# Moving the 28 KB tile of a streamed channel shuffle from the end to fourth place

## The chip, the cores and the metric

One core of one Trainium2 chip. The metric is the device time of one execution in microseconds (us), median over repeated runs. Tile sizes in KB are per partition: "a 38 KB tile" is 128 partitions of 38 KB, 4.98 MB.

## The reference

Within each pixel's 256 channels, 8 groups of 32 are interleaved. The values do not change, only their places.

```python
x = x.reshape(16, 64, 64, 8, 32)      # groups, channels per group
x = x.transpose(0, 1, 2, 4, 3)
return x.reshape(16, 64, 64, 256)     # float32: 67.11 MB in, 67.11 MB out
```

## The kernel before

The tensor is cut into slots; a slot is one tile. SyncE issues the loads, VectorE copies from a load buffer to a store buffer in shuffled order, ScalarE issues the stores. There are two load buffers and three store buffers. The first tile is loaded, copied and stored in three parts (4, 8 and 16 KB).

```python
_SLOTS = [[4, 8, 16]] + [[38]] * 12 + [[28]]
_IN_BUFS = 2
_OUT_BUFS = 3
# ... (pools, shapes)
for parts in _SLOTS:
    in_tile = in_pool.tile([P, biggest * c], F32, name="in_tile")
    out_tile = out_pool.tile([P, biggest * c], F32, name="out_tile")
    # ... (pieces: size, first row, columns)
    for q, start, cols in pieces:
        nc.sync.dma_start(out=in_tile[:, cols], in_=rows(x_flat, start, q))
    for q, start, cols in pieces:
        nc.vector.tensor_copy(
            out=out_tile[:, cols].rearrange("p (i j g) -> p i j g", j=CPG, g=G),
            in_=in_tile[:, cols].rearrange("p (i g j) -> p i j g", g=G, j=CPG),
        )
        nc.scalar.dma_start(out=rows(out_flat, start, q), in_=out_tile[:, cols])
```

Of the kernel before, what the change touches and what calls it, by code (L numbers as in the profile page):

```python
# [1 line left out]

# [4 lines left out]


F32 = mybir.dt.float32
P = 128  # L10

_SLOTS = [[4, 8, 16]] + [[38]] * 12 + [[28]]
_IN_BUFS = 2
_OUT_BUFS = 3


@with_exitstack
def kernel(
    ctx: ExitStack,
    tc: tile.TileContext,  # L20
    x: bass.AP,
    groups: bass.AP,
    out: bass.AP,
):
    nc = tc.nc
    b, h, w, c = x.shape
    G = int(groups)
    CPG = c // G
    assert G * CPG == c
    assert sum(map(sum, _SLOTS)) * P == b * h * w  # L30
    biggest = max(map(sum, _SLOTS))

    x_flat = x.rearrange("b h w c -> (b h w c)")
    out_flat = out.rearrange("b h w c -> (b h w c)")

    in_pool = ctx.enter_context(tc.tile_pool(name="in_pool", bufs=_IN_BUFS))
    out_pool = ctx.enter_context(tc.tile_pool(name="out_pool", bufs=_OUT_BUFS))

    def rows(flat, first, q):

        return flat[first * c : (first + P * q) * c].rearrange("(p f) -> p f", p=P)

    ctx.enter_context(tc.manual_schedule(engines=None))
    first = 0
# [3 lines that stand above are left out]
        at = 0  # L48
        pieces = []
        for q in parts:  # L50
            pieces.append((q, first, slice(at * c, (at + q) * c)))
            first += P * q
            at += q
# [7 lines that stand above are left out]
            nc.scalar.dma_start(  # L61
                out=rows(out_flat, start, q), in_=out_tile[:, cols]
            )


# [1 line left out]
_INS = ['x', 'groups']  # L67
_OUTS = [((16, 64, 64, 256), 'float32')]

_NUMBERS = {'groups': 8}  # L70


# [26 lines left out]
```

## Time and profile before

| | before |
|---|---|
| median of 3 runs | 316.44 us (316.36 to 316.44) |
| profiled span | 314.5 us |
| VectorE busy | 120.0 us, 38% |
| bytes moved | 134.22 MB, mean 427 GB/s |

The profile shows the span in slices with the busy tenths of the DMA engines, the packets of each DMA queue, and the groups of instructions. In the lines of a DMA queue, q1 is the loads and q10 the stores; the columns are packets, MB, and the time that the packets took as a share of 16 engines. Packets are counted where they begin, so a short stretch can show a little over 100%. The lines themselves stand in the prediction.

### The profile page before, as it was taken

The page shows a single profiled execution, that of the slowest core. Times are in us where ns is not written, and L with a number is a line of the kernel's source. Part 1 is how long each engine was busy: PE and PEld are TensorE (multiplying, and loading weights), DVE is VectorE, ACT ScalarE, POOL GpSimd, SP SyncE. Part 2 cuts the span into 40 slices and gives each one's busy share as a digit, 9 for nine tenths or more (in the row PEclk, how much of TensorE's full clock was granted, in tenths as well). Part 3 has the DMA queues.
Part 4 walks back from the last instruction along what each step waited for, and adds up shares of the span by engine and source line. Part 5 has one row for each costly group of instructions (what it writes and reads, how often), then busy time and mean ns, then how long its engine had stood idle before and what let it go on. Part 6 is the DMA issues. An engine that isn't in the chain of part 4 may idle for free.

```text
span 314.5 us, 131 instructions
## 1 busy us (share of the span) xinstructions
DVE 120.0 (38%) x16; POOL 0.2 (0%) x4
## 2 busy tenths in 40 slices
DVE  3407474290280380470560550640730830823400
POOL 0000000000000000000000000000000000000000
DMA  8999999999999999999999999999999999999997
GB/s 315 448 410 445 417 396 479 401 455 416 445 426 436 436 401 470 396 475 396 475 396 475 396 475 396 470 401 455 416 450 421 436 436 411 477 392 454 406 431 343
DMA packets 4609, 134.22 MB, mean 427 GB/s; under 512 B 513, under 2 KB 513, under 8 KB 769
## 3 DMA queue, kind: packets, MB, share of 16 engines
q1 hardware_dynamic: 2304, 67.11, 49.9%
q10 hardware_dynamic: 2304, 67.11, 49.4%
q14 instruction: 1, 0.00, 0.0%
HBM read 67.11 MB, written 67.11 MB: 427 GB/s over the span
## 4 chain that ended last, share of the span: by engine, by line
DMA 74%; DVE 19%; SPq 0%; issue 0%; DVEq 0%
DMA in_tile<-in_x_dram 74%; DVE out_tile L57 19%; SPq L55 0%; DVEq L57 0%
## 5 line engine op out<-in xcount | busy, mean ns | idle before, releaser
L57 DVE COPY out_tile<-in_tile 128x9728 f32<-128x9728 f32 (+4 forms) x16 | 120.0, 7501 | 174.7 <-DMA in_tile<-in_x_dram 174.7
L80 POOL MEMSET const-bfloat16-1.0<- 128x1 bf16 x1 | 0.1, 102 | 0.0
L80 POOL MEMSET const-uint8-127<- 128x1 uint8 x1 | 0.1, 102 | 0.0
L80 POOL MEMSET const-float32-0.0<- 128x1 f32 x1 | 0.1, 99 | 0.2 <-issue 0.2
L80 POOL MEMSET const-float32-1.0<- 128x1 f32 x1 | 0.1, 99 | 0.0
## 6 DMA issues: line engine op xcount, KB each, us to landing
in_tile<-in_x_dram SPq DMA_DIRECT2D x12, 4864.0 KB, 36.9
out_dram<-out_tile ACTq DMA_DIRECT2D x12, 4864.0 KB, 48.2
in_tile<-in_x_dram SPq DMA_DIRECT2D x1, 3584.0 KB, 33.9
out_dram<-out_tile ACTq DMA_DIRECT2D x1, 3584.0 KB, 19.0
in_tile<-in_x_dram SPq DMA_DIRECT2D x1, 2048.0 KB, 10.9
out_dram<-out_tile ACTq DMA_DIRECT2D x1, 2048.0 KB, 33.2
in_tile<-in_x_dram SPq DMA_DIRECT2D x1, 1024.0 KB, 5.4
out_dram<-out_tile ACTq DMA_DIRECT2D x1, 1024.0 KB, 24.2
```

The lines of the kernel that those rows point to most:

```text
L57: nc.vector.tensor_copy(out=out_tile[:, cols].rearrange("p (i j g) -> p i j g", j=CPG, g=G), in_=in_tile[:, cols].rearrange("p (i g j) -> ...
L80: nc = _bacc.Bacc("TRN2", target_bir_lowering=False, num_devices=1)
```

## The change

The intent: with a smaller tile in the second load buffer, that buffer is copied out sooner and its next load is issued sooner. The sizes, and so the bytes, stay the same; one load, one copy and one store move from last to fourth.

```diff
-_SLOTS = [[4, 8, 16]] + [[38]] * 12 + [[28]]
+_SLOTS = [[4, 8, 16], [28]] + [[38]] * 12
```

## The prediction

> **What bounds the kernel now.** I read the page first: the busy shares, the DMA queues and the issues.
>
> ```profile
> span 314.5 us, 131 instructions
> DVE 120.0 (38%) x16; POOL 0.2 (0%) x4
> DMA  8999999999999999999999999999999999999997
> ...
> q1 hardware_dynamic: 2304, 67.11, 49.9%
> q10 hardware_dynamic: 2304, 67.11, 49.4%
> ```
>
> The reader is to see that VectorE, the only compute engine at work, is idle for 62% of the span, while the DMA row is full from the first slice to the last. Loads (q1, issued by SyncE) and stores (q10, issued by ScalarE) each take half of the 16 DMA engines: 49.9 + 49.4 = 99.3% of the span. Each queue has 2304 packets for 16 transfers, 144 a transfer: 128 rows (one per partition) and 16 tiny ones. So a row of a tile is one packet whatever its size, and each DMA engine gets 8 rows of each transfer.
>
> Then the table of stretches, to see where the missing 0.7% lies (columns: stretch, its length, VectorE busy, GpSimd busy, clock, DMA share, GB/s).
>
> ```profile
> 0.00:1.72 1.72, 0.00 (x0) 0.20 (x4) 1.00 0.00 0
> 1.72:313.40 311.68, 120.01 (x16) 0.00 (x0) 1.00 1.00 431
> 313.40:314.50 1.10, 0.00 (x0) 0.00 (x0) 1.00 0.00 0
> 61.20:268.00 206.80, 79.85 (x9) 0.00 (x0) 1.00 1.00 434
> ```
>
> It lies at the two ends: 1.72 us before the first packet and 1.10 us after the last. Between them the share is 1.00. The DMA engines are the bound, and there is no hole in the middle to be closed.
>
> The page's chain says "DMA in_tile" 74% and the copies 19%. It follows the last copy backwards through the two load buffers and does not show that those loads stood in a full queue, so I do not read the copies as a cost. The timeline of the copies, start and last, with what they waited for:
>
> ```profile
> 12.60 3.87 DVE L57 COPY out_tile<-in_tile 128x4096 f32<-128x4096 f32 x1 [4.04 <-DMA in_tile<-in_x_dram]
> 25.93 8.95 DVE L57 COPY out_tile<-in_tile 128x9728 f32<-128x9728 f32 x1 [9.47 <-DMA in_tile<-in_x_dram]
> 41.57 8.87 DVE L57 COPY out_tile<-in_tile 128x9728 f32<-128x9728 f32 x1 [6.68 <-DMA in_tile<-in_x_dram]
> 61.31 8.87 DVE L57 COPY out_tile<-in_tile 128x9728 f32<-128x9728 f32 x1 [10.87 <-DMA in_tile<-in_x_dram]
> ...
> 288.10 6.58 DVE L57 COPY out_tile<-in_tile 128x7168 f32<-128x7168 f32 x1 [11.17 <-DMA in_tile<-in_x_dram]
> ```
>
> Every copy begins when its load lands and none waits for a store (the view of waits has no such entry). At the end, the view of DMA issues for the last 60 us gives 28.2 us to landing for the last 38 KB store and 19.0 us for the 28 KB one. They were issued at 276.96 and 294.70 (the end of their copies), so they landed at 305.2 and 313.7: the last store stood behind the one before it for 10.5 us.
>
> **What the Trainium skill says.** (1) "DMA: Bandwidth & Descriptors", section "Queues, rings and completion order": each DMA engine goes round the queues that have work, one whole packet from each. This trace agrees. In a steady stretch of one period (93.1 to 116.1 us) the DMA view counts the same packets for both queues:
>
> ```profile
> q1 hardware_dynamic: 144, 4.98, 50.1%
> q10 hardware_dynamic: 144, 4.98, 50.1%
> ```
>
> and from 12.6 to 25.9 us, where loads have 38 KB rows and stores 4 and 8 KB rows, again 144 each, though bytes differ:
>
> ```profile
> q1 hardware_dynamic: 144, 4.98, 86.9%
> q10 hardware_dynamic: 144, 0.85, 15.3%
> ```
>
> So loads and stores advance row against row, not byte against byte. (2) The same page, "Where 436 GB/s comes from": a ceiling of 435.2 GB/s for these 16 engines. The trace's steady 434 is at it, so no rate is left to win. (3) "SBUF — State Buffer", section "SBUF: two separate sides": a DMA is not slowed by a compute operation. The trace agrees as far as it goes: DMA share 1.00 with VectorE busy 39% of that stretch.
>
> **The change part by part.** Nothing is removed or added: the same 16 loads, copies and stores of the same sizes, the same two load and three store buffers; the instruction order moves one copy, one load and one store from last to fourth.
>
> *Cost of a row.* 50.1% of 16 x 23.0 us over 128 rows is 1.44 us for a 38 KB row. In the stretch 276 to 277 us, 16 rows of 28 KB took 106.2% of 16 us, 1.06 us each. The moved tile is 8 + 8 rows on each DMA engine, 17.0 us, before and after. Sum: 0.
>
> *The start.* Landing times here and below are the issue times of the timeline plus the time to landing of the DMA view over short windows. The 16 KB load lands at 12.6. Before, the next load (38 KB) landed at 25.9. After, it has 28 KB rows: 8 x (1.44 - 1.06) = 3.0 us less, with the same 8 small store rows between, so about 22.9. Its copy takes 6.6 us in place of 8.95: done near 29.6, not 34.9. So the second buffer is free, and its next load issued, 5.3 us sooner. That is the intent, and it comes true. But the load for the first buffer was issued at 16.5, when the 16 KB copy ended, and it occupies the queue: from 25.9 to 41.55 before (15.6 us), from 22.9 to 38.5 after. The sooner load waits in the queue 8.9 us (38.5 - 29.6) where it waited 6.6 (41.55 - 34.9). Nothing was starving; the head start is spent standing in line. Gain: 0.
>
> *The middle.* Period 23.0 us, as before; loads all land some 3 us earlier, because 3 us of load work has not left the queue's total but stores now do it later. How far stores lie behind loads is kept in rows. The seventh load landed at 84.2, and the fourth and fifth stores at 72.65 and 95.67, so 4.5 stores were through: a lag of 2.5 transfers, 20 rows per engine. The first three transfers each way (4, 8 and 16 KB) set this lag, and they do not change. A store buffer is reused after three tiles: before, the store issued at 93.1 landed 48.5 us later, at 141.6, and the copy that needs its buffer began at 153.3, a margin of 11.7 us. The tightest new place, the fourth copied tile, needs the 16 KB store landed. That comes near 38.5 + 4 x (1.44 + 0.61) = 46.7, against a load landing near 56.7 (19.7 us after the last before, now less 4 x 0.38 for four 28 KB store rows). No wait appears. Cost: 0.
>
> *The end.* With the last load landed, 20 store rows remain per engine. Before: 12 x 1.44 + 8 x 1.06 = 25.8 us, measured 288.0 to 313.7. After: 20 x 1.44 = 28.8 us, so the last load must land near 313.7 - 28.8 = 284.9. Its copy takes 8.9 and ends near 293.8. The 12 rows ahead of its store last until 284.9 + 17.3 = 302.2. The longer last copy therefore still has 8.4 us to spare (10.5 before). Cost: 0.
>
> Sum: 0, so 316.4 us, the median of before.
>
> **The rivals.** *A serial end.* If the last load, copy and store were a bare chain, the larger last tile would cost 8.9 - 6.6 = 2.3 us of copy and 8 x 0.38 = 3.0 us of store: 321.7. Against it: the stores waiting in front of the last one; the DMA share while the last copy ran (288.0 to 294.7) is 1.06, so full. *A starved load queue at the start.* If the engines sat idle until the second buffer came free, up to 5.3 us would be won: 311.1. Against it: from 12.6 to 25.9 the two queues' shares sum to 102%, and from 25.9 to 41.5 to 97.5%, so at most 0.4 us is there. *A store-buffer wait takes over.* If the lag grew by more than 4 rows, copies would wait for stores; the load queue would drain, yet the stores would run in its place, so it costs little unless both queues are empty. Nothing lengthens the lag: 316 to 318. *The edges of the transfers.* Larger rows at the very end can leave the 16 engines finishing less evenly, by up to one row's difference, 0.4 us; small rows pair otherwise at the start: 316.8.
>
> **Range and chances.** Three runs of before span 0.08 us. The edges are worth about 0.4 us either way, and another sitting may differ by as much, so 316.4 with 315.6 to 317.2. Two per cent is 6.3 us: more than the idle of both ends together, and to lose as much the last copy would have to lie bare. Faster 0.01, same 0.98, slower 0.01.
>
> **What would show it right or wrong.** Right: DMA share 1.00 from about 1.7 us to about 1 us before the end, 2304 packets a queue; the fourth copy starts near 22.9 and takes 6.6; its buffer's next load is issued near 29.6 and lands near 56.7; the last copy starts near 285 and ends near 294; still no copy waits for a store. Wrong: a DMA slice below 9 in the middle or during the last copy, a copy waiting for out_dram, or a row of 38 KB that takes another time than 1.44 us.

## The result, and the profile after

After: median 316.4 us (316.21 to 316.45, 6 runs); before in the same rounds 316.4 us (316.26 to 316.72, 6 runs). The ratio is 0.9998, 95% interval 0.9985 to 1.0011: the same.

The page of after, first its busy shares, DMA row and queues:

```profile
span 314.7 us, 131 instructions
DVE 119.4 (38%) x16; POOL 0.2 (0%) x4
DMA  8999999999999999999999999999999999999997
...
q1 hardware_dynamic: 2304, 67.11, 49.8%
q10 hardware_dynamic: 2304, 67.11, 49.4%
```

Nothing that bounds the kernel has moved: the DMA row is the same digit for digit, and the two queues still fill the span. The timeline of the copies of after (start, length, what ended the idle time before) shows what did move:

```profile
12.76 3.88 DVE L57 COPY out_tile<-in_tile 128x4096 f32<-128x4096 f32 x1 [4.31 <-DMA in_tile<-in_x_dram]
23.09 6.59 DVE L57 COPY out_tile<-in_tile 128x7168 f32<-128x7168 f32 x1 [6.45 <-DMA in_tile<-in_x_dram]
38.75 8.78 DVE L57 COPY out_tile<-in_tile 128x9728 f32<-128x9728 f32 x1 [9.07 <-DMA in_tile<-in_x_dram]
56.97 8.94 DVE L57 COPY out_tile<-in_tile 128x9728 f32<-128x9728 f32 x1 [9.44 <-DMA in_tile<-in_x_dram]
...
285.28 8.83 DVE L57 COPY out_tile<-in_tile 128x9728 f32<-128x9728 f32 x1 [14.19 <-DMA in_tile<-in_x_dram]
```

The second buffer was free at 29.7 us instead of 34.9. Its next load was issued there and landed at 56.9; before, issued 5.2 us later, it landed at 61.2. From the seventh load to the fifteenth, each lands 5.8 us sooner than the same load in order of before: some 3 us because the fourth load has 28 KB rows, and some 3 us because the eight rows of the 28 KB store now stand between them. The last load has 38 KB rows again and gives 3 us back (its copy starts at 285.3, before at 288.1). And the last store lands at 313.9 us, before at 313.7: the rest is paid back in the stretch of stores alone at the end, which has one 38 KB store where a 28 KB one stood.

The table of stretches of after (stretch, length, VectorE busy, GpSimd busy, clock, DMA share, GB/s) shows that no hole opened, not during the last copy either (packets that began just before a stretch are not counted in it, so 0.98 is still full):

```profile
1.72:313.50 311.78, 119.41 (x16) 0.00 (x0) 1.00 1.00 430
285.30:294.10 8.80, 8.80 (x1) 0.00 (x0) 1.00 0.98 425
```

And the DMA view of one steady period of after (110.2 to 133.2 us), with the time from issue to landing of the one load and the one store issued in it:

```profile
q1 hardware_dynamic: 144, 4.98, 50.1%
q10 hardware_dynamic: 144, 4.98, 50.1%
...
in_tile<-in_x_dram SPq DMA_DIRECT2D x1, 4864.0 KB, 37.1
out_dram<-out_tile ACTq DMA_DIRECT2D x1, 4864.0 KB, 48.5
```

These are the figures of before (37.0 and 48.5): both are issued when a copy ends, and a store lands 11.4 us, half a transfer, after a load. That half transfer turned out to matter, as the experiments show.

### The profile page after: what moved, and what is told of

It is laid out like the page before. It is cut to its first block, busy times and chain, and to the rows that moved or that the text cites. A ratio compares the mean times of both kernels' runs of the same rounds, so it can differ in the third digit from the quotient of the medians.

```text
span 314.7 us, 131 instructions
## 1 busy us (share of the span) xinstructions
DVE 119.4 (38%) x16; POOL 0.2 (0%) x4
## 4 chain that ended last, share of the span: by engine, by line
DMA 74%; DVE 19%; SPq 0%; issue 0%; DVEq 0%
DMA in_tile<-in_x_dram 74%; DVE out_tile L57 19%; SPq L55 0%; DVEq L57 0%
## 5 line engine op out<-in xcount | busy, mean ns | idle before, releaser
L57 DVE COPY out_tile<-in_tile 128x9728 f32<-128x9728 f32 (+4 forms) x16 | 119.4, 7463 | 174.7 <-DMA in_tile<-in_x_dram 174.7
```

The source lines that it names most:

```text
L57: nc.vector.tensor_copy(out=out_tile[:, cols].rearrange("p (i j g) -> p i j g", j=CPG, g=G), in_=in_tile[:, cols].rearrange("p (i g j) -> ...
```

## The experiments

The theory: the DMA engines are full from 1.7 us to the end, so the order of tiles is free as long as neither end lies bare. Rival A: the zero is a gain at the start and an equal loss at the end. Rival B: the last load, copy and store are a bare chain. Rival D: the start is on the path, as the intent of the change has it. All medians below stand against 316.3 us of before on the same chip, taken in the same rounds.

### The two halves of the change apart

`e1_end_only` has the start of before and the end of after; `e2_start_only` has the start of after and the end of before.

```diff
 # e1_end_only
-_SLOTS = [[4, 8, 16]] + [[38]] * 12 + [[28]]
+_SLOTS = [[4, 8, 16]] + [[38]] * 6 + [[28]] + [[38]] * 6
 # e2_start_only
+_SLOTS = [[4, 8, 16], [28]] + [[38]] * 5 + [[10]] + [[38]] * 6 + [[28]]
```

> The start of before with the end of after: the 28 KB tile stands in the middle (eighth), the 38 KB ones last. Theory (the DMA engines are full, order is free): 316.4 us, within 0.5 of before; the last copy 8.8 us, starting near 285. Rival A (the sooner second buffer won some us and the larger last tile lost as many, so the change's zero is a sum of two): slower than before by what the start was worth, 3 to 5 us. Rival B (bare serial end): 321.7.

> The start of after with the end of before: 4, 8, 16, then 28 KB in the second buffer, one 38 KB tile cut into a 10 KB tile in the middle and a 28 KB tile at the end. Theory: 316.4 us, at most 0.5 more for the extra 10 KB rows. Rival A (gain at the start, loss at the end): faster than before by 3 to 5 us, since only the gain is left.

Measured: 316.30 us (ratio 1.0006, interval 0.9992 to 1.0020) and 316.46 us (1.0012, 1.0000 to 1.0025). Neither half is worth anything by itself; rival A, which needs 3 to 5 us on each side, falls. In `e1_end_only` the last copy started at 285.1 us and took 8.8, as said.

### How much the end can bear

The last copy is done twice. The result stays right; only the last store is issued later.

```diff
+            for _ in range(2 if t == len(_SLOTS) - 1 else 1):
                 nc.vector.tensor_copy(...)
```

> Before with its last copy (28 KB, 6.6 us) done twice, result unchanged. Theory (reserve at the end): the copy then ends at 294.7 + 6.6 = 301.3, while store rows in front of it last until about 304.5, so nothing is lost: 316.4 to 316.9. Rival B (the last copy is bare): plus 6.6, 323.

> After with its last copy (38 KB, 8.8 us) done twice, result unchanged. Theory: the copy ends at 294.1 + 8.8 = 302.9, the rows in front of its store ran out near 301.7; with about 1 us from issue to first row the engines idle some 2 us: plus 1.5 to 3.5, so 318 to 320. Rival B (bare): plus 8.8, 325. Rival C (the end is covered whatever is done): plus 0.

Measured: on before 316.38 us (ratio 1.0005, 0.9990 to 1.0020), on after 318.34 us (1.0066, 1.0051 to 1.0081). The timeline and two stretches of the second:

```profile
285.19 17.80 DVE L58 COPY out_tile<-in_tile 128x9728 f32<-128x9728 f32 x2 [14.23 <-DMA in_tile<-in_x_dram]
...
1.72:302.00 300.28, 127.31 (x17) 0.00 (x0) 1.00 1.00 430
301.70:303.90 2.20, 1.28 (x1) 0.00 (x0) 1.00 0.29 124
```

The rows in front of the last store run out at 301.7 us, while the copy ends at 303.0 and the first row of its store begins at 303.9 (counted from the packets): some 2.2 us without work, and only there does the DMA share fall. Of 8.8 us more copy, 2.1 us show, so the reserve at the end of after is 6.7 us; of 6.6 us more on before, none. Rival B asked for all of it, rival C for none. So the end has a reserve in both kernels, and the change makes it smaller: it uses up some of what was free.

### How much the copies weigh

The shuffle is left out (wrong result), which makes every copy of after faster.

```diff
-                out=out_tile[:, cols].rearrange("p (i j g) -> p i j g", j=CPG, g=G),
-                in_=in_tile[:, cols].rearrange("p (i g j) -> p i j g", g=G, j=CPG),
+                out=out_tile[:, cols], in_=in_tile[:, cols]
```

> Wrong result on purpose: after with the copies in plain order, no shuffle, so VectorE writes with unit steps. Theory: whatever the copies then take (perhaps half of 8.8 us, perhaps the same), the time stays 316.4 within 0.4, because copies lie beside full DMA queues. Rival (the chain's 19% of copies is on the path): faster by the copies saved, up to 6 us if the first and last count, up to 50 us if the whole 19% does.

```profile
L57 DVE COPY out_tile<-in_tile 128x9728 f32<-128x9728 f32 x12 | 62.7, 5227 | 201.8 <-DMA in_tile<-in_x_dram 201.8
```

That line is the group of the twelve large copies in this run: 62.7 us in all, 5227 ns of one, where after has 8.7 to 9.0 us. The time was 316.66 us (ratio 1.0011, 0.9998 to 1.0025). Some 50 us of VectorE work taken away are worth nothing. The 19% that the page's chain gives to the copies are no cost.

### How much the start can bear

The copy out of the second load buffer is made longer: by 2.9 us on after (12 of its 28 KB copied again), by its full length on before and on after.

```diff
 # e12_after_second_late
+            for part in [cols, slice(0, 12 * c)] if t == 1 else [cols]:
 # e5_before_second_x2, e6_after_second_x2
+            for _ in range(2 if t == 1 else 1):
                 nc.vector.tensor_copy(...)
```

> After with 12 of the 28 KB copied twice in the second buffer's tile: 2.9 us of delay, its buffer free at 32.6 in place of 29.7, with a measured 2.3 us from issue to the first row 34.9, before the load queue runs out (36.5 to 37.8). Theory (slack at the start): no row is delayed, the lag stays 20 rows, 316.4 within 0.5. Rival D (the start is on the path): plus 2.9. Rival F (any disturbance of the start upsets the phase): plus 10 or more.

> Before with the copy out of the second buffer (38 KB, 8.9 us) done twice. Theory: the buffer is free at 34.9 + 8.9 = 43.8; the load queue runs out at 40.6 and the 16 KB store rows left, at full rate, at about 43.0; some 2 us idle: plus 1 to 3.5. Rival D (the start is on the path, as the change intends): plus 8.9. Rival E (start of no account at all): plus 0.

> After with the copy out of the second buffer (28 KB, 6.6 us) done twice. Theory: free at 29.7 + 6.6 = 36.3, before the load queue runs out at 37.8: plus 0 to 0.4. Together with the run on before: the change buys slack at the start and no time. Rival D (on the path): plus 6.6.

`e12_after_second_late` took 316.32 us (1.0004, 0.9991 to 1.0016). Its buffer's next load was issued at 32.66 us, so more than half of the 5.2 us won by the change was given away at no price. That is direct evidence against rival D.

The two full doublings went wrong for the theory and for every rival: 330.17 us on before (1.0436), 338.66 us on after (1.0731), more than the added copy itself (8.9 and 6.6 us). The table of stretches of `e5_before_second_x2` tells where:

```profile
42.00:47.00 5.00, 5.00 (x2) 0.00 (x0) 1.00 0.73 197
60.00:268.00 208.00, 74.82 (x9) 0.00 (x0) 1.00 1.00 413
```

The hole that I had expected is there, from 42 to 47 us: by this view 1.4 us of idle engines (27% of 5), and 1.8 us if each packet is counted for as long as it lasts. But the loss goes on for the rest of the run: DMA share 1.00 and yet 413 GB/s, where before has 434. Over 208 us that is 208 x (1 - 413/434) = 10 us. The DMA view of one period (119.1 to 143.1 us) shows in what:

```profile
q10 hardware_dynamic: 144, 4.98, 52.6%
q1 hardware_dynamic: 144, 4.98, 48.0%
...
in_tile<-in_x_dram SPq DMA_DIRECT2D x1, 4864.0 KB, 39.2
out_dram<-out_tile ACTq DMA_DIRECT2D x1, 4864.0 KB, 39.4
```

A store row takes 52.6% of 16 x 24.0 us over 128 rows, 1.58 us, in place of 1.44; a load row still 1.44. And load and store now land together (39.2 and 39.4 us after a common issue), where before they land 11.4 us apart. While the load queue was empty, the stores caught up from 20 rows behind the loads to 16, exactly two transfers.

In `e6_after_second_x2` I had the reserve too large. The copy ended at 37.7 us (the load before it had landed at 24.5, in after at 23.1), the next load was issued at once, and yet the DMA view from 39 to 40 us has not one load packet:

```profile
DMA packets 23, 0.38 MB, mean 377 GB/s; under 512 B 0, under 2 KB 0, under 8 KB 0
...
q10 hardware_dynamic: 23, 0.38, 87.8%
```

The first row of that load came at 40.0 us, 2.3 us after its issue; I had allowed about 1. Meanwhile the stores, at 0.61 us for a 16 KB row, ran the same four rows ahead. From there on the loads and stores of this run land together as well. It loses more than `e5_before_second_x2` partly at its end: while its last copy ran (311.2 to 320.0 us) the DMA share was 0.50, some 4 us of idle engines. With the stores four rows nearer and the engines no longer level, the reserve at the end is used up too; how much each of the two adds is not shown.

### A coarser start

> The 4, 8 and 16 KB first tile is replaced by one of 28 KB; 28, twelve of 38, 28. Theory in numbers: each DMA engine has 2 x (96 rows of 1.439 + 16 rows of 1.062 us) = 310.3 us of rows against 312.2 us measured for before (99.3% of 314.5), so about 1.9 us less: 314.5, range 314.2 to 315.4, although the first store can only begin near 18 us and not at 9. Rival (small first tiles are needed so that stores begin early): slower by up to 9 us.

```diff
-_SLOTS = [[4, 8, 16]] + [[38]] * 12 + [[28]]
+_SLOTS = [[28]] + [[38]] * 12 + [[28]]
```

I hoped for a version that beats both kernels, since every small row carries some extra. Measured: 328.43 us (ratio 1.0393, 1.0372 to 1.0415). The rival, that late first stores leave the engines idle, is not what the profile shows: the start is full. Its stretches, and its DMA view of one period (92.3 to 116.44 us):

```profile
1.72:36.00 34.28, 15.44 (x2) 0.00 (x0) 1.00 1.02 422
60.00:268.00 208.00, 77.25 (x9) 0.00 (x0) 1.00 1.00 414
```

```profile
q10 hardware_dynamic: 144, 4.98, 52.3%
...
in_tile<-in_x_dram SPq DMA_DIRECT2D x1, 4864.0 KB, 39.3
out_dram<-out_tile ACTq DMA_DIRECT2D x1, 4864.0 KB, 39.5
```

It is the same picture as above with no copy delayed and no queue dry: stores 16 rows behind, both landing together, store rows of 1.58 us.

### Three attempts to set the phase on purpose

The new theory: what counts, beside full engines, is the phase between the two queues. When the rows of a load and of a store run in step, store rows are slower. To move the phase alone, I cut one transfer into pieces over fewer partitions, so that each DMA engine gets a few rows more for the same bytes.

```diff
 # e9_coarse_shifted: the first load of the coarse start; e10_before_shifted: the store of tile 3
+cuts = [(0, 64, 0, half), (0, 64, half, n), (64, P, 0, n)]   # partitions, columns
 # e11_ladder: the stores of tiles 3, 5, 7 and 9
+cuts = [(0, 16, 0, half), (0, 16, half, n), (16, P, 0, n)]
```

> The coarse start (28, twelve of 38, 28) again, but its first load is cut into three pieces that give each DMA engine 12 rows in place of 8, the same bytes. New theory (phase): in the slow runs so far loads and stores cross a transfer's border together, 16 rows apart, and store rows take 1.58 us in place of 1.44; four more load rows put the stores 20 rows behind, as before and after have it, so store rows go back to 1.44, the period from 24.1 to 23.0 and the time to 314.2 to 315.6. Rival (the late first stores, or the missing small tiles, cost the time): stays near 328.

> Before with the store of its fourth tile cut into three pieces (12 rows per engine in place of 8, same bytes). No copy is delayed and no queue runs dry. Phase theory: from there on stores are 16 rows behind, store rows take 1.58 us, nine periods of 24.1 in place of 23.0: plus 9 to 12, so 325 to 329. Rival (the doubled copies lost their time by idle engines alone): 316.4 to 317.

> Before with one more store row per engine at each of the tiles 3, 5, 7 and 9 (a store cut so that an engine has 9 rows), so stores are 20, 19, 18, 17 and 16 rows behind in turn. Phase theory: store rows take 1.44 us in the first stage and 1.58 in the last; what they take at 19, 18 and 17 is not known: if only the exact meeting of rows counts they stay at 1.44 until the last stage, so plus 2 to 4; if nearness counts they rise step by step, plus 5 to 8. Rival (no phase effect): 1.44 throughout, 316.4 to 317.

None of the three gave the clean test. `e9_coarse_shifted` ran from 324.79 to 343.24 us (its profile is of a slow run). Its first load crawled. The DMA view of its first 12 us, then that of `e8_coarse_start` in the same 12 us:

```profile
DMA packets 177, 2.32 MB, mean 194 GB/s; under 512 B 32, under 2 KB 32, under 8 KB 32
```

```profile
DMA packets 160, 4.29 MB, mean 358 GB/s; under 512 B 16, under 2 KB 16, under 8 KB 16
```

Half the rate with half the partitions: the Trainium skill states it ("SBUF — State Buffer", section "Door 1: The DMA port swizzle": partitions 0 to 63 reach only half of the DMA ports), and this run agrees, 194 against 358 GB/s. With that slow start the phase that I wanted did not come about; the landings, which wait for the slowest of the 16 engines, came together here too.

`e10_before_shifted` took 321.54 us (1.0165, 1.0152 to 1.0178), between the two expectations, and so confirms neither. Its stores ended 2.7 to 2.9 us, one pair of rows, behind a load's landing, not in step, and its store rows stayed at 1.44. My expectation had the direction wrong: more store rows put the stores further behind, toward 24 rows and not 16. A load and a store issued together (at 160.5 us) land 35.0 and 60.8 us later, 25.8 us or 9 pairs of rows apart: 25 rows, one past three whole transfers. About 2 of the 5.2 us lost went while the cut pieces ran (418 GB/s from 85 to 140 us, in before 435); the rest is not placed. `e11_ladder`, one run at 331.07 us, mixes several phases with slow 16-partition pieces; nothing follows from it.

What the runs show together, counted from the packets of each trace (38 KB rows begun between 130 and 250 us; the gap is from the landing of a load, that is of its slowest engine, to the next landing of a store):

| run | gap, us | store rows over 1.5 us | median, us |
|---|---|---|---|
| before, after | 11.3 to 11.5 | 0% | 316.4 |
| `e4_after_last_x2` | 13.1 to 13.2 | 0% | 318.3 |
| `e12_after_second_late` | 11.3 to 11.5 | 0% | 316.3 |
| `e7_plain_copy` | 10.3 to 10.5 | 0% | 316.7 |
| `e10_before_shifted` | 2.7 to 2.9, once 5.2 | 0% (5.5% of load rows) | 321.5 |
| `e8_coarse_start` | 0.2 | 93% | 328.4 |
| `e5_before_second_x2` | 0.2 | 99.5% | 330.2 |
| `e6_after_second_x2` | 0.2 | 65% | 338.7 |
| `e9_coarse_shifted` | 0.2 | 5.5% | 324.8 to 343.2 |

In every run of the table whose transfers land together, some or nearly all store rows are slow; with a gap over 10 us none is. The pages of these runs say where the time went (a queue's share times the span): against before, the stores take 10.4 us more of each engine's time in `e5_before_second_x2`, 10.6 in `e8_coarse_start` and 11.0 in `e6_after_second_x2`, of 13.8, 11.6 and 20.4 us more span. In the last, loads take 3.2 us more as well, and 6.2 us more are idle.

Two runs hold a control within them. The packets do not name their engine, but each begins within 5 ns of the end of another, so they can be strung into 16 chains, one for each engine (where two packets end together the chains can be swapped, so a few rows are put to the wrong one). In `e8_coarse_start`, 15 engines have a load and a store cross the border of a transfer together, and 573 of their 576 store rows between 130 and 250 us are slow. The 16th crosses them a row or two apart; of the 59 rows outside the step 39 are not slow, nearly all of them one engine's. In `e9_coarse_shifted` it is the other way round: one engine is in step, with 35 of 44 store rows slow; the other 15 cross a row or two apart, with 2 slow rows of 625. That one engine's transfers take 24.1 us where the first to finish need 23.0, and at the end the rest wait for it. So in the same run, at the same time and with the same tiles, the engines that are in step have the slow store rows; a row or two out of step is enough to be free of them (in `e10_before_shifted`, one row out, 5.5% of the load rows are slow instead).

**What stays open.** The link between phase and slow store rows rests on these comparisons, between runs of different make and between the engines of two runs (the profile of `e9_coarse_shifted` is of a run classed slow); no run set the phase and nothing else. Nor do the runs tell whether the two rows meet in the same SBUF partitions or in HBM. A later test should shift the phase with full 128-partition transfers, by the sizes of the first tiles.

## Why the prediction was right, point by point

*The bound.* It held: DMA share 1.00, steady 433 GB/s in after. `e7_plain_copy` shows it from the other side, with VectorE's work cut from 119.4 to 70.8 us and the time unchanged.

*The start.* Predicted for the fourth copy 22.9 us and 6.6 long, for the next load 29.6, for its landing 56.7. Measured 23.1, 6.59, 29.7 and 56.9. `e2_start_only` and `e12_after_second_late` confirm that the head start has no price. The slack, however, is bounded, and below it lies a cliff that the prediction did not see.

*The middle.* The period is 23.0 us and no copy waits for a store. One statement was off: the loads land 5.8 us earlier from the seventh on, not "some 3 us"; the eight 28 KB store rows, which the estimate of 56.7 counts in part, were left out of it. Nothing rested on it, since the last load again has 38 KB rows. The prediction said that the lag of 20 rows is set by the first three transfers and does not change. That was right, and it was the step that bore the most weight: with a gap of 11.4 us in both kernels, store rows stay at 1.44 us. I had thought of the lag only as room in the store buffers. Its rival "a store-buffer wait takes over" spoke of a longer lag and found it cheap unless both queues are empty; a shorter one, 16 rows, cost over 10 us with full queues in `e5_before_second_x2` and `e8_coarse_start`. Had the change moved the lag to 16 rows, the time would have been some 4% longer, as in these two, and by the prediction's own working nobody would have seen why. That the lag is kept was reasoned; that 20 rows is a good one was luck.

*The end.* Predicted: last copy near 285 to 294, 8.4 us to spare until the store rows in front of it end at 302.2. Measured: 285.3 to 294.1, the store before the last landed at 302.4. `e4_after_last_x2` uses the reserve up and then pays 2.1 us, in the range of 1.5 to 3.5 expected from it. So the mechanism held and the reserve was a little too large: 6.7 us in place of 8.4, since the rows ran out at 301.7 and a store's first row begins 0.9 us after its copy ends.

*The chances.* Both medians lie at 316.4 us, and the ratio's interval is within 0.2% of one. The reason given for "slower 0.01", that for a loss of 2% the last copy would have to lie bare, does not hold: `e5_before_second_x2` lost 13.9 us with a DMA share of 1.08 during its last copy (307.7 to 314.3 us).

## What to carry to other kernels

Where the DMA share is 1.00 from end to end, a load issued sooner only waits longer in its queue: look for idle DMA time before you reorder, and test both ends apart, for two nothings are a stronger finding than one zero. Before you call a start or an end free, measure its reserve by lengthening one copy until it shows. And compare not only the DMA share but the time per row: engines at 1.00 moved 434 GB/s in one kernel and 413 in another, and the sign to look for was loads and stores landing together.

## What the Trainium skill lacked or had wrong

- "DMA: Bandwidth & Descriptors", section "Queues, rings and completion order", has the round-robin between queues right (144 packets each in a period) but nothing on rows in step: in four runs whose loads and stores land within 0.2 us of each other, up to 99.5% of the 38 KB store rows take about 1.58 us in place of 1.44, and in `e5_before_second_x2` and `e8_coarse_start` the period is near 24.1 us in place of 23.0. Engines of the same run that are not in step keep 1.44. Where the two rows meet is not known.
- The same page, section "Latency and other measured facts", gives some 600 ns from a sync or scalar queue's issue to the first byte. With the other queue busy, the load issued at 37.7 us in `e6_after_second_x2` had its first row at 40.0, 2.3 us later. With both queues empty, the first load of before had its first row 1.0 us after its issue began (0.73 to 1.72), and the last store of `e4_after_last_x2` 0.9 us.
